# Two conv tiles instead of three by accumulating transfers, and most weight remainders on GpSimd

## Chip, core and metric

The kernel runs on one core of one Trainium2 chip. The metric is device time in microseconds (us) of one execution; the figure for the kernel is the median of three runs. A core has five engines with queues of their own: TensorE (PE in the profile; PEld is its loading of weights), VectorE (DVE), ScalarE (ACT), GpSimd (POOL) and SyncE (SP, which issues transfers here). An engine takes its instructions in the order in which the program gives them and waits, on semaphores, for what they need.

## What is computed

One layer of a decoder trunk on a sequence of 1024 tokens of width 1024, in float32:

```python
h = rmsnorm(x, norm_g[l]) * (1.0 + scale[:, None, :]) + shift[:, None, :]
u = h @ w_in[l]
cv, cg, cs, lx, ls = jnp.split(u, [D_CONV, 2*D_CONV, 3*D_CONV, 3*D_CONV + D_LRU], axis=-1)

v = cv * jax.nn.sigmoid(cg)
v = causal_depthwise_conv(v, dw_w[l], dw_b[l])            # 31 taps
v = jax.nn.silu(layernorm(v, cln_g[l], cln_b[l]))         # over all 1024 channels
y_conv = (v @ pw2_w[l] + pw2_b[l]) * jax.nn.silu(cs)
...
y = jnp.concatenate([y_conv, y_lru], axis=-1) @ w_out[l]
x = x + (1.0 + gate[:, None, :]) * y
return rmsnorm(x, final_g)
```

The left-out part is the second group: a 4-tap conv, two gates from block-diagonal products, and a linear recurrence over the tokens. `scale`, `shift` and `gate` come from a product of the condition `c` with `mod_w`.

## The kernel before

**Tiles.** Channels lie on the 128 partitions and tokens along the free axis, so a tensor of 1024 channels is eight tiles of 128 x 1024. Products use the fast float32 format of TensorE in three parts: each operand is split into a rounded value (`h`, by a cast on ScalarE) and what is left of it (`l`, by a subtraction), and TensorE adds h·h, h·l and l·h. For a weight tile these are `whi` and `wlo`. The subtraction that makes `wlo` is the *remainder* of the title. One weight tile of the middle takes 48 matmuls of 512 columns.

**Stages.** First the modulation and the products of the first four weight tiles (`first`), then the other 36 tiles of `w_in` mixed with the eight heads' gates, then the eight recurrence tiles of `w_out` (`lru`), while the LayerNorm of the conv group runs beside them; then the pointwise product (`pw2`, a scheme of seven products for eight) and the rest of `w_out`, and the final norm. TensorE's share of the conv group begins only with `pw2`, after the LayerNorm.

**Order.** No engine's order is written by hand. `Plan.op` collects each operation with an engine, an estimated cost and a priority (lower first); `Plan.order` plays them through one clock: whenever an engine is free it takes the ready operation with the lowest priority. The order in which they were taken is then emitted and is fixed. The planner also models that VectorE and GpSimd share a port: `o.lock` marks every GpSimd operation that is no transfer, and every VectorE operation that doesn't read PSUM; two such operations are not put at the same time (`held`). An operation's `lock` on VectorE is `not in_psum(r)` (L371, L377).

**Weights.** `weights` (L496) loads a weight tile with priority n - 2.5 and hands it to `w_slice` (L479), which casts it on ScalarE and subtracts with `SUB` (L384, a `TT`, L373) with priority n - 1.4, n being the tile's number. `whi` and `wlo` have two buffers each, so a tile can be prepared once TensorE has finished the one before the last. Tiles below `EARLY` = 11 that aren't in `LOP` have their remainder on GpSimd (these are 8, 9 and 10), the others on VectorE.

**Conv tiles.** `conv_tile` (L1085, priority 1000 + 5i, behind everything else) makes the 31 taps by a scheme of even and odd positions with 15, 14 and 14 plus 1 multiply-adds (`STT`, L366), each with one operand in SBUF and the accumulator (`cacc`, `caccs`) in PSUM, on VectorE. A tile whose number is in `POOLED` goes to `conv_pooled` (L1136) instead: ScalarE makes the products (`cq`, `co`), and GpSimd adds them up by transfers that accumulate in memory (`ADD`, L379, into `es` and `oo`). Both forms end with three additions of half tiles on VectorE. `conv_sum` (L1172) adds the eight results to `csum`, in the order 2, 6, 1, 4, 3, 0, 7, 5, and not before weight tile 38 has begun; the LayerNorm starts from it.

The rule by which the order is found, at its core (L248):

```python
k = (o.prio + (2.0 if o.table and o.table != table else 0.0), o.seq)
if key is not None and k >= key:
    continue
```

Of the kernel before, what the change touches and what calls it, by code (L numbers as in the profile page):

```python
# [9 lines left out]
F32 = mybir.dt.float32  # L10
F32R = mybir.dt.float32r
AF = mybir.ActivationFunctionType
ALU = mybir.AluOpType
# [31 lines left out]
ZK = 3  # L45
UK = 7
HRES = 6
POOLED = (1, 3, 5)
TLATE = 2
QGATES = ((2, 5), (3, 0), (3, 2), (3, 2))  # L50
CSUM = 38
# [30 lines left out]
SP0 = 1.0  # L82
SPP = 25
PAD = 16
GLO = 'DVE'
GDOT = 'DVE'
FOLD = 'DVE'
# [28 lines left out]

class Op:
    __slots__ = ("eng", "cost", "emit", "prio", "table", "bufs", "succ", "wait", "ready",
                 "seq", "reserve", "columns", "lock", "end", "psum", "lag", "slack")


class Plan:
# [23 lines left out]
    def op(self, eng, cost, emit, prio, r=(), w=(), table=None, after=(), reserve=0,  # L146
           columns=0, lock=False, lag=0.0, slack=0.0):
        o = Op()
        o.lag, o.slack = lag, slack
        o.eng, o.cost, o.emit, o.prio, o.table = eng, cost, emit, prio, table  # L150
        o.succ, o.ready, o.seq, o.reserve = [], 0.0, len(self.ops), reserve
        o.columns = columns
        o.lock = not lag and eng == "POOL" or eng == "DVE" and lock
        r, w = list(self.keys(r)), list(self.keys(w))
        preds = set(after)
        for k in r:
            if k in self.writer:
                preds.add(self.writer[k])
        for k in w:
            if k in self.writer:  # L160
                preds.add(self.writer[k])
            preds.update(self.readers.get(k, ()))
        for k in r:
            self.readers.setdefault(k, []).append(o)
        for k in w:
            self.writer[k] = o
            self.readers[k] = []
        preds.discard(o)
        o.wait = len(preds)
        for p in preds:  # L170
            p.succ.append(o)
        o.bufs = list(dict.fromkeys(k[0] for k in r + w if isinstance(k[0], Buf)))
        for b in o.bufs:
            b.left += 1
        o.psum = [(b, any(k[0] is b for k in w)) for b in o.bufs if b.pool == "bank"]
        self.ops.append(o)
        return o

    def order(self):
# [10 lines left out]
        waiting = None  # L190
        left = len(self.ops)

        def clear(o):
# [36 lines left out]
        while left:  # L230
            while releases and releases[0][0] <= t:
                free[heapq.heappop(releases)[2]] += 1
            moved, later = False, []
            if waiting and held["DVE"] <= t + 1e-9:
                o, waiting, moved = waiting, None, True
                held["POOL"] = t + o.cost
                done(o, t + o.cost)
            for e in engines:
                if until[e] > t + 1e-9:
                    continue  # L240
                best, key = None, None
                for o in pending[e]:
                    if o.ready > t + 1e-9:
                        continue
                    if e == "DVE" and o.lock and held["POOL"] > t + 1e-9:
                        later.append(held["POOL"])
                        continue
# [12 lines left out]
                    best, key = o, k  # L260
                if best is None:
# [12 lines left out]
                end = t + cost  # L274
                out.append((t, o))
                for b in o.bufs:
                    if b.pool in free and b not in live:
                        live.add(b)
                        free[b.pool] -= 1
                if e == "POOL" and o.lock and held["DVE"] > t + 1e-9:  # L280
                    waiting, until[e] = o, float("inf")
                    continue
                if o.lock:
                    if e == "DVE":
                        end = max(t, held["POOL"]) + cost
                    held[e] = end
                done(o, end)
            if not moved:
                nxt = later + [u for u in until.values() if t + 1e-9 < u < float("inf")]
                nxt += [o.ready for e in engines for o in pending[e] if o.ready > t + 1e-9]  # L290
                if releases:
                    nxt.append(releases[0][0])
                assert nxt, "no operation can go on"
                t = min(nxt)
        return out

    def run(self):
        for _, o in self.order():
            for b in o.bufs:
                if b.tile is None:  # L300
                    pool, tag, shape, _ = self.pools[b.pool]
                    b.tile = pool.tile(shape, b.dtype, tag=tag, name=b.name)
            o.emit()


@with_exitstack
def hymba_layer(ctx: ExitStack, tc: tile.TileContext, xT, xa, vecs, mod_w, mod_s0, w_first, w_pairs, w_in,
# [21 lines left out]
    for n in ("u", "s", "s2", "q", "r"):  # L329
        pools["sp_" + n] = (small, "sp_" + n, [P, KT], 1)  # L330
    S = Plan(pools)


    def a_cost(n, ptr=0):
# [30 lines left out]

    def STT(prio, out, in0, scalar, in1, op0, op1, n=T, accum=None, r=(), w=(), after=()):  # L366
        def emit():
            dve.scalar_tensor_tensor(out=out(), in0=in0(), scalar=scalar, in1=in1(), op0=op0,  # L368
                                     op1=op1, accum_out=accum)
        return S.op("DVE", d_cost(n, not isinstance(scalar, float)), emit, prio, r, w,  # L370
                    lock=not in_psum(r), after=after)  # L371

    def TT(prio, eng, out, a, b, op, n=T, r=(), w=(), reserve=0, after=()):  # L373
        e = dve if eng == "DVE" else pool
        return S.op(eng, d_cost(n) if eng == "DVE" else p_cost(n),
                    lambda: e.tensor_tensor(out=out(), in0=a(), in1=b(), op=op), prio, r, w,  # L376
                    reserve=reserve, lock=not in_psum(r), after=after)  # L377

    def ADD(prio, out, a, n=T, r=(), w=(), after=()):  # L379

        return S.op("POOL", ISSUE, lambda: pool.dma_start(out(), a(), accum_op=ALU.add), prio, r,  # L381
                    w, lag=RATE * n / T, after=after)

    def SUB(prio, eng, lo, full, hi, n=T, r=(), w=(), reserve=0):  # L384
        return TT(prio, eng, lo, full, lambda: hi().bitcast(F32), ALU.subtract, n, r, w, reserve)
# [683 lines left out]
    def tap_sums(pr):  # L1069
        def emit():  # L1070
            t = V[:, DWW:].rearrange("p (i s) -> p i s", s=TAPS)[:, :, 1:]
            t = t.rearrange("p i (q z) -> p i q z", z=2)
            dve.tensor_tensor(out=wsum.rearrange("p (i q) -> p i q", q=15), in0=t[:, :, :, 0],
                              in1=t[:, :, :, 1], op=ALU.add)
# [583 lines left out]
```

## Time and profile before

| | |
|---|---|
| median of three runs | 726.26 us (726.0 to 726.36) |
| the profiled execution: span from first to last instruction | 724.4 us |
| instructions | 8887 |
| TensorE busy | 717.0 us, 99% |
| VectorE busy | 638.9 us, 88% |
| ScalarE busy | 474.2 us, 65% |
| GpSimd busy | 86.6 us, 12% |
| mean granted TensorE clock | 0.997 |
| TensorE's stages, by the chain that ended last | first weights 8.4 to 47 us; middle to 557; pointwise 557 to 633; output to 718 |
| bytes by GpSimd's transfer queue | 34.26 MB of 111.58 MB |

The span is of one execution, and the time of a run is somewhat longer than it (by 1.9 us here). "Busy" is the union of an engine's instructions; those of TensorE overlap, as a matmul of 512 columns is shown with 389 ns while one begins every 227 ns. A row of a group reads: line, engine, operation, output <- inputs, shapes, count | busy us, mean ns | idle time of the engine before them <- what ended it. Lines are often those of a helper (L368 is `STT`, L376 `TT`, L357 and L349 `ACT`, L381 `ADD`).

### The profile page before, as it was taken

What the parts mean: (1) busy time and instruction counts of PE and PEld (TensorE: products, weight loads), DVE (VectorE), ACT (ScalarE), POOL (GpSimd) and SP (SyncE); (2) the same over time, 40 slices, a digit from 0 to 9 for tenths busy, and PEclk for the clock granted to TensorE, in tenths of its full rate; (3) what the DMA queues carried; (4) which work ended last, traced back from release to release, by engine and by line L of the source; (5) the groups of instructions that cost most, each with busy time, mean ns of one, the idle gap of its engine ahead of it and who ended that gap; (6) DMA issues with size and microseconds to landing.
All of it is one profiled execution on the core that took longest, in us unless ns stands there. A gap on an engine that the chain in (4) does not pass through costs nothing.

```text
span 724.4 us, 8887 instructions
## 1 busy us (share of the span) xinstructions
PE 717.0 (99%) x3236; PEld 596.9 (82%) x3236; DVE 638.9 (88%) x907; ACT 474.2 (65%) x659; POOL 86.6 (12%) x101
## 2 busy tenths in 40 slices
PE   9999999999999999999999999999999999999996
PEld 7888888888888888888888888888888888888886
DVE  6999999999999988688899995998999766997757
ACT  6675765777787977957867895835764334645443
POOL 0001012121231332233121100000000000000001
PEclk9999999999999999999999999999999999999998
DMA  9960024397799799799884536243332530433116
GB/s 342 407 234 29 30 92 104 83 202 181 172 237 235 149 216 222 148 217 210 187 178 90 105 89 195 88 175 138 124 117 86 205 111 6 159 108 140 59 57 233
DMA packets 36475, 111.58 MB, mean 154 GB/s; under 512 B 4048, under 2 KB 10960, under 8 KB 36432
## 3 DMA queue, kind: packets, MB, share of 16 engines
q1 hardware_dynamic: 23616, 76.36, 29.3%
q0 software_dynamic: 12528, 34.26, 26.3%
q8 instruction: 25, 0.41, 0.2%
q10 hardware_dynamic: 288, 0.39, 0.1%
q14 instruction: 18, 0.15, 0.1%
HBM read 64.16 MB, written 12.58 MB: 106 GB/s over the span
## 4 chain that ended last, share of the span: by engine, by line
PE 99%; DVE 0%; ACT 0%; issue 0%; DVEq 0%
PE ps L508 66%; PE first L807 5%; PE pupw L619 3%; PE papw L619 3%; PE gate L1247 3%; PE pbpw L619 3%; PE out L689 2%; PE puout L619 2%; PE paout L619 2%; PE pcpw L619 2%; PE pb0out L619 1%; PE pcout L619 1%; PE late L807 1%; PE out6b L689 1%; PE c_row L759 1%; PE pb1out L619 0%
## 5 line engine op out<-in xcount | busy, mean ns | idle before, releaser
L508 PE MATMUL ps<-uh,whi 128*128 128x512 f32 x576 | 224.2, 389 | 0.0
L508 PE MATMUL ps<-ul,whi 128*128 128x512 f32 x576 | 224.1, 389 | 0.0
L508 PE MATMUL ps<-uh,wlo 128*128 128x512 f32 x576 | 224.1, 389 | 0.0
L508 PEld LDWEIGHTS ps<-uh,wlo 128*128 128x128 f32 x576 | 108.1, 188 | 22.5
L508 PEld LDWEIGHTS ps<-ul,whi 128*128 128x128 f32 x576 | 108.1, 188 | 22.4
L508 PEld LDWEIGHTS ps<-uh,whi 128*128 128x128 f32 x576 | 108.1, 188 | 22.3
L349 ACT CAST whi<-raw 128x1024 fp32r<-128x1024 f32 x46 | 48.1, 1049 | 41.8 <-PE ps L508 34.7
L376 DVE TENSOR_TENSOR wlo<-raw,whi 128x1024 fp32r<-128x1024 f32 x43 | 52.5, 1221 | 17.0 <-ACT whi L349 16.7
L357 ACT ACT_TABLE_LOAD x47 | 60.3, 1283 | 3.6 <-issue 1.5
L381 POOL DMA_DIRECT2D es<-cq x45 | 40.3, 908 | 165.8 <-ACT cq L357 118.5
L368 DVE SCALAR_TENSOR_TENSOR cacc<-v,V,cacc 128x511 f32<-128x511 f32 (+14 forms) x75 | 55.8, 744 | 0.4
L368 DVE SCALAR_TENSOR_TENSOR caccs<-v,V,caccs 128x511 f32<-128x511 f32 (+6 forms) x70 | 52.2, 745 | 1.2
L368 DVE SCALAR_TENSOR_TENSOR caccs<-c,wsum,caccs 128x511 f32<-128x511 f32 (+6 forms) x70 | 52.1, 745 | 0.6
L508 PE MATMUL ps<-yh,wlo 128*128 128x512 f32 x128 | 49.8, 389 | 0.0
L508 PE MATMUL ps<-yl,whi 128*128 128x512 f32 x128 | 49.8, 389 | 0.0
L508 PE MATMUL ps<-yh,whi 128*128 128x512 f32 x128 | 49.8, 389 | 0.0
L381 POOL DMA_DIRECT2D oo<-co x42 | 38.7, 921 | 82.5 <-ACT co L357 39.6
L368 DVE SCALAR_TENSOR_TENSOR xs<-ps,V,xs 128x512 f32<-128x512 f32 (+3 forms) x48 | 35.9, 747 | 0.8 <-ACT xs L357 0.5
L376 POOL TENSOR_TENSOR fg<-fg,bc 128x512 f32<-128x512 f32 x2 | 2.5, 1278 | 276.9 <-ACT bc L349 276.9
L357 ACT ACTIVATE cq<-v,V 128x511 f32<-128x511 f32 (+14 forms) x45 | 31.8, 708 | 0.0
L357 ACT ACTIVATE cq<-c,wsum 128x512 f32<-128x512 f32 x42 | 29.6, 714 | 0.0
L357 ACT ACTIVATE co<-v,V 128x511 f32<-128x511 f32 (+13 forms) x42 | 29.4, 708 | 0.0
(387 smaller groups left out, 1441.9 us busy)
## 6 DMA issues: line engine op xcount, KB each, us to landing
raw<-in_w_in_dram SPq DMA_DIRECT2D x36, 512.0 KB, 5.1
modw<-in_mod_w_dram SPq DMA_DIRECT2D x23, 512.0 KB, 8.8
raw<-in_w_out_dram SPq DMA_DIRECT2D x10, 512.0 KB, 4.0
scsd<-scs SPq DMA_DIRECT2D x8, 512.0 KB, 4.0
acc<-in_xT_dram SPq DMA_DIRECT2D x8, 512.0 KB, 4.4
accd<-acc SPq DMA_DIRECT2D x8, 512.0 KB, 2.6
rawpw<-in_pw_dram SPq DMA_DIRECT2D x8, 512.0 KB, 3.2
scsr<-scsd SPq DMA_DIRECT2D x8, 512.0 KB, 4.9
```

The costliest lines, as they stand in the source:

```text
L349: act.copy(out(), in_())
L357: act.activation(out=out(), in_=in_(), func=func, **kw)
L368: dve.scalar_tensor_tensor(out=out(), in0=in0(), scalar=scalar, in1=in1(), op0=op0, op1=op1, accum_out=accum)
L376: lambda: e.tensor_tensor(out=out(), in0=a(), in1=b(), op=op), prio, r, w,
L381: return S.op("POOL", ISSUE, lambda: pool.dma_start(out(), a(), accum_op=ALU.add), prio, r, w, lag=RATE * n / T, after=after)
L508: pe.matmul(part(ps, a - off, b - off)(), k3(lhs)()[:, k, :], rhs[k]()[:, a:b], start=(k == 0 and lhs is wh and rhs is xh and (a - off) % ...
L619: pe.matmul(part(ps, 0, c1 - c0)(), half(*lhs)()[:, j * P:j * P + P], half(*rhs)()[:, c0:c1], start=start and j == 0 and z == 0, stop=j == ...
L689: pe.matmul(part(ps, a - off, e - off)(), k3(lhs)()[:, k, :], rhs()[:, i * H + a % H:i * H + a % H + e - a], start=k == KORD[0] and lhs is ...
L759: pe.matmul(part(ps_c[z], k * P - a, k * P - a + P)(), cs[:, k:k + 1].to_broadcast([P, P]), ident, start=True, stop=True)
L807: pe.matmul(part(ps, a - off, b - off)(), fw_part(lhs, k, i * P, i * P + P)(), rhs()[:, a:b], start=k == 0 and lhs is wh and rhs is xh, st ...
L1247: pe.matmul(ps(), lhs()[:, j, :], rhs()[:, c0:c1], start=st == 0, stop=st == 2)
```

## The change

`POOLED` becomes (2, 4): conv tiles 1, 3 and 5 go to VectorE, 2 and 4 to the transfers. The remainders whose preparation priority lies from 6 to 46 are marked `pooled` with GpSimd's cost. When the planner picks for VectorE, such an operation counts as one that GpSimd may take: for the first 5 us after it is ready VectorE leaves it alone, and GpSimd gets it as soon as GpSimd is free, VectorE's next operation is one that reads PSUM, and the PSUM-reading work at hand lasts at least 0.7 of GpSimd's cost. It is then made to wait for the VectorE operation before that stretch (`behind`, a dependency for the order alone). After the 5 us VectorE may take it as before.

```diff
-POOLED = (1, 3, 5)
+POOLED = (2, 4)
...
+DEFER, RUNS = 5.0, 0.7
+PW0, PW1 = 6, 46
+SYNC = mybir.DependencyInfo(mybir.DependencyClass.Sync, mybir.DependencyReason.SCHED_ONLY)
...
 class Op:
...
+    def run(self):
+
+        n, o = 0.0, self
+        while o is not None:
+            n += o.cost
+            o = next((s for s in o.succ if s.eng == "DVE" and not s.lock and s.wait == 1), None)
+        return n
...
-                best, key = None, None
+                best, key, flex, run = None, None, [], 0.0
                 for o in pending[e]:
                     if o.ready > t + 1e-9:
                         continue
+                    if o.pooled and held["POOL"] <= t + 1e-9:
+                        flex.append(o)
+                        if t + 1e-9 < o.ready + DEFER:
+                            later.append(o.ready + DEFER)
+                            continue
...
                     best, key = o, k
+                    if e == "DVE" and not o.lock:
+                        run += o.run()
+                if flex and best is not None and not best.lock and until["POOL"] <= t + 1e-9 \
+                        and not waiting:
+                    o = min(flex, key=lambda o: (o.prio, o.seq))
+                    if run >= RUNS * o.pooled:
+                        o.eng, o.cost, o.behind = "POOL", o.pooled, previous
+                        pending[e].remove(o)
...
+                        held["POOL"] = t + o.cost
+                        done(o, t + o.cost)
...
+                if e == "DVE":
+                    previous = o
...
-            o.emit()
+            o.ins = o.emit()
+            if o.behind:
+                self.tc.add_manual_dep(o.ins.ins, o.behind.ins.ins.name, SYNC, reason="shared port")
...
-    def TT(prio, eng, out, a, b, op, n=T, r=(), w=(), reserve=0, after=()):
+    def TT(prio, eng, out, a, b, op, n=T, r=(), w=(), reserve=0, after=(), pooled=False):
+        def emit():
+            return (dve if o.eng == "DVE" else pool).tensor_tensor(out=out(), in0=a(), in1=b(), op=op)
...
+        if pooled and eng == "DVE":
+            o.pooled = p_cost(n)
+        return o
...
-        SUB(LOP.get(p_load + 2.5, p_prep), eng, cut(lo), cut(rw), cut(hi), n, r=keys(rw) + keys(hi), w=keys(lo))
+        SUB(LOP.get(p_load + 2.5, p_prep), eng, cut(lo), cut(rw), cut(hi), n, r=keys(rw) + keys(hi),
+            w=keys(lo), pooled=PW0 <= p_prep <= PW1)
```

The rest of the diff lets the helpers return the instruction that they emit.

More of the change, by code (lines that the diff above doesn't have):

```diff
@@ L118 @@
     __slots__ = ("eng", "cost", "emit", "prio", "table", "bufs", "succ", "wait", "ready",
-                 "seq", "reserve", "columns", "lock", "end", "psum", "lag", "slack")
+                 "seq", "reserve", "columns", "lock", "end", "psum", "lag", "slack", "pooled",
+                 "behind", "ins")
+    def run(self):
[4 more added lines that the diff above has]
+        return n
 class Plan:
@@ L148, in op @@
         o = Op()
-        o.lag, o.slack = lag, slack
+        o.lag, o.slack, o.pooled, o.behind, o.ins = lag, slack, None, None, None
         o.eng, o.cost, o.emit, o.prio, o.table = eng, cost, emit, prio, table
@@ L189, in order @@
         held = {"DVE": 0.0, "POOL": 0.0}
-        waiting = None
+        waiting, previous = None, None
         left = len(self.ops)
@@ L260, in order @@
                     best, key = o, k
+                    if e == "DVE" and not o.lock:
[6 more added lines that the diff above has]
+                        pending[e].remove(o)
+                        left -= 1
+                        out.append((t, o))
+                        for b in o.bufs:
+                            if b.pool in free and b not in live:
+                                live.add(b)
+                                free[b.pool] -= 1
+                        held["POOL"] = t + o.cost
+                        done(o, t + o.cost)
                 if best is None:
@@ L331, in hymba_layer @@
     S = Plan(pools)
+    S.tc = tc
     def a_cost(n, ptr=0):
@@ L367, in emit @@
         def emit():
-            dve.scalar_tensor_tensor(out=out(), in0=in0(), scalar=scalar, in1=in1(), op0=op0,
-                                     op1=op1, accum_out=accum)
+            return dve.scalar_tensor_tensor(out=out(), in0=in0(), scalar=scalar, in1=in1(),
+                                            op0=op0, op1=op1, accum_out=accum)
         return S.op("DVE", d_cost(n, not isinstance(scalar, float)), emit, prio, r, w,
                     lock=not in_psum(r), after=after)
-    def TT(prio, eng, out, a, b, op, n=T, r=(), w=(), reserve=0, after=()):
[L374 to L377, printed above, removed]
+    def TT(prio, eng, out, a, b, op, n=T, r=(), w=(), reserve=0, after=(), pooled=False):
+        def emit():
+            return (dve if o.eng == "DVE" else pool).tensor_tensor(out=out(), in0=a(), in1=b(), op=op)
+        o = S.op(eng, d_cost(n) if eng == "DVE" else p_cost(n), emit, prio, r, w,
+                 reserve=reserve, lock=not in_psum(r), after=after)
+        if pooled and eng == "DVE":
+            o.pooled = p_cost(n)
+        return o
     def ADD(prio, out, a, n=T, r=(), w=(), after=()):
```

9 lines of the change are left out of this document (5 added, 4 removed).

## The prediction

> **What bounds the kernel now.** I read the table of windows first, cut where TensorE's state changes: before its first large product, the long middle, the last products, and what follows them. Columns: the window, its length, then busy time and instructions of PE, PEld, DVE, ACT and POOL, the granted TensorE clock, the DMA share and GB/s.
>
> ```profile
> 0.00:8.40 8.40, 6.80 (x31) 6.43 (x31) 2.95 (x14) 4.71 (x9) 0.70 (x6) 1.00 0.77 260
> 8.40:700.00 691.60, 691.60 (x3057) 572.55 (x3058) 618.74 (x859) 458.11 (x621) 83.36 (x93) 1.00 0.56 152
> 700.00:718.30 18.30, 18.30 (x151) 17.88 (x149) 14.63 (x30) 11.34 (x31) 2.53 (x2) 1.00 0.38 142
> 718.30:724.40 6.10, 0.27 (x3) 0.08 (x1) 2.55 (x5) 0.00 (x0) 0.00 (x0) 0.70 0.72 266
> sum 724.40, PE 716.97 PEld 596.93 DVE 638.87 ACT 474.15 POOL 86.59; mean PE 179.24 PEld 149.23 DVE 159.72 ACT 118.54 POOL 21.65
> ```
>
> The reader is to see that TensorE is busy for all of the 691.60 us of the middle, at clock 1.00, and then for all 18.30 us of the last products. "Busy" alone would not prove it, since the ends of matmuls are modelled, so the second view is that of the waits of PE, with the sum, the number and the longest:
>
> ```profile
> PE token_stats L754 <- DVE ones L441: 1.1, 1, 1.1
> PE first L807 <- ACT fhi L349: 0.5, 1, 0.5
> ```
>
> Only two waits are listed, 1.6 us together, both before the middle begins. Nothing that VectorE, GpSimd or a DMA does between 8.4 and 700 us makes TensorE wait. **The kernel is bound by the number of matmuls.** The change adds none, removes none and leaves their sizes. What another order of the other engines could win lies in the first 8.4 us and the last 6.1 us, and neither the conv tiles nor the remainders with a preparation priority of 6 to 46 run there. VectorE at 88% looks like a second bound, but an engine with no one waiting for it can give up work without shortening anything.
>
> **The change part by part.** The rows of the page's groups that carry the sizes (count, busy time, mean of one in ns, idle before it):
>
> ```profile
> L376 DVE TENSOR_TENSOR wlo<-raw,whi 128x1024 fp32r<-128x1024 f32 x43 | 52.5, 1221 | 17.0 <-ACT whi L349 16.7
> ...
> L368 DVE SCALAR_TENSOR_TENSOR cacc<-v,V,cacc 128x511 f32<-128x511 f32 (+14 forms) x75 | 55.8, 744 | 0.4
> L368 DVE SCALAR_TENSOR_TENSOR caccs<-v,V,caccs 128x511 f32<-128x511 f32 (+6 forms) x70 | 52.2, 745 | 1.2
> L368 DVE SCALAR_TENSOR_TENSOR caccs<-c,wsum,caccs 128x511 f32<-128x511 f32 (+6 forms) x70 | 52.1, 745 | 0.6
> ...
> L357 ACT ACTIVATE cq<-v,V 128x511 f32<-128x511 f32 (+14 forms) x45 | 31.8, 708 | 0.0
> ```
>
> And GpSimd's own groups, with shapes kept apart:
>
> ```profile
> L381 POOL DMA_DIRECT2D es<-cq x45 | 40.3, 908 | 165.8 <-ACT cq L357 118.5 <-DMA oo<-co 20.3 <-issue 11.5
> L381 POOL DMA_DIRECT2D oo<-co x42 | 38.7, 921 | 82.5 <-ACT co L357 39.6 <-issue 11.1 <-DMA es<-cq 10.6
> L376 POOL TENSOR_TENSOR wlo<-raw,whi 128x1024 fp32r<-128x1024 f32 x3 | 7.2, 2408 | 98.4 <-ACT whi L349 98.4
> ```
>
> *1. One conv tile more on VectorE.* The loop of `conv_tile` issues 15+15+14 multiply-adds a tile, the odd one of which (`caccs<-c,V`) is in a smaller group: 44 x 0.745 = 32.8 us added to VectorE. The four whole-tile passes around them (the sum of even and odd positions and three folds) exist in both forms of the tile: 0.
>
> *2. One tile fewer by accumulating transfers.* GpSimd issues 15 + 14 = 29 fewer of them: 15 x 0.908 + 14 x 0.921 = 26.5 us off GpSimd, and a third of that queue's bytes go. ScalarE loses the 47 products of a tile and gains 3 starts of an accumulator: 44 x 0.708 = 31.2 us off. Both engines were off the path, so the sum takes nothing for this; the cover is TensorE's gapless middle.
>
> *3. Remainders to GpSimd.* `weights` makes remainders 7 to 47 in the main loop; 8 to 10 are on GpSimd already, 7 has a preparation priority of 5.6 and stays, so 37 may move. Each takes 1.22 us from VectorE and costs GpSimd 2.41 us: at most 45.1 us off and 89.1 us on. GpSimd then holds 86.6 - 26.5 + 89.1 = 149 us of 724: no bound. A planner rule sends a remainder back to VectorE when it has waited 5 us, so I take 25 to 33 as moved.
>
> *VectorE's balance.* What matters is the time up to the channel sum that the LayerNorm needs. Windows by the arrivals of conv tiles, then the sum row of the same windows for the tile wlo alone:
>
> ```profile
> 98.00:248.00 150.00, 150.00 (x664) 124.20 (x663) 145.75 (x222) 111.85 (x149) 34.90 (x39) 1.00 0.69 162
> 248.00:362.00 114.00, 114.00 (x505) 94.39 (x504) 92.89 (x121) 88.61 (x124) 32.83 (x38) 1.00 0.95 199
> 362.00:438.00 76.00, 76.00 (x337) 62.94 (x336) 75.38 (x93) 58.09 (x75) 13.12 (x15) 1.00 0.54 116
> 438.00:477.00 39.00, 39.00 (x174) 32.30 (x173) 30.49 (x29) 26.37 (x30) 0.00 (x0) 1.00 0.48 152
> ```
>
> ```profile
> sum 379.00, PE 204.46 PEld 98.53 DVE 37.85 POOL 4.82; mean PE 51.12 PEld 24.63 DVE 9.46 POOL 1.21
> ```
>
> VectorE idles 4.25 + 21.11 + 0.62 + 8.51 = 34.5 us there, and does 37.85 us of remainders. With all moved the balance is 32.8 - 37.9 = -5 us; with three quarters, +4 us; with none, +32.8 us, which the idle time would still just hold. The timeline shows what the sum waited for:
>
> ```profile
> 438.06 1.28 DVE L376 TENSOR_TENSOR c<-c,caccs 128x512 f32<-128x512 f32 x2
> ...
> 476.03 1.22 DVE L376 TENSOR_TENSOR csum<-csum,c 128x1024 f32<-128x1024 f32 x1
> ```
>
> VectorE's last tile was done at 439; the sum ended at 477 because tile 5 came late by the transfers. Now tile 5 is VectorE's and the transfers carry 2 and 4, which arrive earlier, so I expect the sum at 455 to 477. An earlier sum moves work to other places of a middle that TensorE fills anyway: 0. What is late next is again the matmul count.
>
> *4. The added wait.* Each moved remainder waits on GpSimd behind a VectorE instruction. Behind it in GpSimd's order stand the accumulating transfers' issues and later remainders; for the former only tiles 2 and 4 wait, for the latter TensorE. This is where the change can cost, and these rows give the room: a cast, the remainder that follows it, the first matmul with it.
>
> ```profile
> 201.41 1.05 ACT L349 CAST whi<-raw 128x1024 fp32r<-128x1024 f32 x1 [4.43 <-PE ps L508]
> ...
> 212.77 0.39 PE L508 MATMUL ps<-uh,wlo 128*128 128x512 f32 x1
> ...
> 432.61 1.06 ACT L349 CAST whi<-raw 128x1024 fp32r<-128x1024 f32 x1 [0.39 <-PE ps L508]
> ...
> 436.92 1.22 DVE L376 TENSOR_TENSOR wlo<-raw,whi 128x1024 fp32r<-128x1024 f32 x1
> ...
> 470.37 1.06 ACT L349 CAST whi<-raw 128x1024 fp32r<-128x1024 f32 x1
> ...
> 479.33 0.39 PE L508 MATMUL ps<-yh,wlo 128*128 128x512 f32 x1
> ```
>
> From the end of a cast (202.46) to the first use (212.77) there are 10.3 us; in the tightest place I found (471.43 to 479.33) 7.9. The planner lets a remainder wait up to 5 us, and GpSimd needs 2.4: 7.4 at worst, which leaves 2.9 us typically and 0.5 at the tightest place. On top comes how far the chip runs behind the plan: the remainder at 436.92 began 3.3 us after its cast although its priority is high, because VectorE's fixed order had other work first. The bounds of this step are therefore 0 (no remainder late) and about 3.3 - 0.5 = 2.8 us (the tightest one late by the largest lag). It is no sum over remainders: TensorE, once delayed, delays the next use as well, so only the largest excess counts. I take 0, since it needs a full wait, the tightest place and the largest lag together.
>
> *5. GpSimd beside VectorE.* The planner keeps the two apart unless VectorE reads PSUM. The one case of before inside a stretch of VectorE work:
>
> ```profile
> 54.78 3.67 DVE L376 TENSOR_TENSOR first_u<-first,rbc 128x512 f32<-128x512 f32 x6
> ...
> 55.66 2.40 POOL L376 TENSOR_TENSOR wlo<-raw,whi 128x1024 fp32r<-128x1024 f32 x1 [54.36 <-ACT whi L349]
> ```
>
> Six instructions in 3.67 us (0.61 apiece) while GpSimd took its usual 2.40: neither slowed, and `first` is in PSUM. The conv multiply-adds too have one operand in PSUM and one in SBUF, so I price the overlap at 0. No row shows GpSimd beside a VectorE instruction with both operands in SBUF; bounds: 0, and one whole remainder, 2.4 us of VectorE, each time. [...]
>
> **Sum.** 0 + 0 + 0 + 0 + 0 on the profiled execution: span 724.4 us. The median of the runs is 726.26, so 1.86 us lie around the span, and I leave them: **726.3 us**.
>
> **Rivals.**
>
> *A. A remainder comes late (slower).* GpSimd's queue holds a remainder behind an issue that waits for ScalarE's product (those waits are the 118.5 us of the row above), and TensorE waits for it. For: the reserve of 0.5 to 2.9 us against a lag of up to 3.3. Against: ScalarE loses 31 us of work and a third of the issues go. It decides from the point where wait + lag pass 7.9 us at the tightest or 10.3 us at the usual place. Price 1.6 to 4 us: 728 to 730.
>
> *B. GpSimd and VectorE exclude each other often (slower).* If the real order drifts, each moved remainder can stop VectorE for up to 2.4 us. VectorE has 34.5 us of room, less the balance of -5 to +4: from about 13 to 16 full stops on, the channel sum passes 477 and TensorE runs dry before the pointwise products. At 18 stops, 43 us, it is 4 to 13 us over: 730 to 739. [...]
>
> *C. The end is laid out anew (faster).* The planner is one pass over all operations, so another state at 560 us could reorder the last 24 us. There TensorE leaves 6.1 - 0.27 = 5.8 us; were a quarter of it and the 0.5 us wait won, 724.3. Against: of the 72.9 us that VectorE idles in the middle window (691.60 - 618.74) at most 34.5 lie between 98 and 477 us; in the rest, most of it after the channel sum, a difference of the two orders should have died out.
>
> *D. Few remainders move.* If the planner seldom finds the PSUM stretch, VectorE carries the tile alone: +32.8 against 34.5 us of room. The time is again 726.3, with the sum later.
>
> **How the numbers follow.** Forecast 0.62 and D 0.10 both stay within 0.2% (1.45 us; about what a measurement can tell): same 0.72. A 0.15 and B 0.06: slower 0.21. C: faster 0.07. The range reaches from 725.2, a little under the lowest run (726.0), to 729.5, which takes in most of A; left out are B, C and the end of A, about 0.16. The likeliest case's own range is 725.6 to 727.2.
>
> **What would show it.** Right: PE's waits still list no more than the two at the start, the middle window still 691.6 of 691.6, while wlo shows 28 to 36 instructions on POOL at about 2.4 us, the conv groups grow to 90, 84 and 84, and the issues fall to 30 and 28. Wrong by A: a wait of PE on POOL wlo. By B: wlo on POOL, or VectorE's two-operand groups, with means well over 2.4 and 1.22 us, and the sum later than 477. By C: a shorter stretch after 700 us with the same middle.

## The result, and the profile after

On one chip, nine runs of each: 725.83 us before (725.48 to 726.36), **727.74 us after** (727.68 to 728.35). The ratio is 1.0026, with a 95% interval of 1.0018 to 1.0035: slower by 1.9 us, just over what a measurement of this kernel can tell from no change. The time lies in the predicted range, on the side to which I had given 0.21. One run of the kernel before (801 us) and two of a kernel below (802 and 1037 us) came out far longer at a lower granted clock (0.85, 0.85 and 0.65) and are left out of all medians and ratios here.

What was meant to move did move. The page of after, first its busy line, then its groups:

```profile
PE 716.0 (99%) x3236; PEld 595.6 (82%) x3236; DVE 647.0 (89%) x923; ACT 447.5 (62%) x615; POOL 137.5 (19%) x99
...
L413 POOL TENSOR_TENSOR wlo<-raw,whi 128x1024 fp32r<-128x1024 f32 x31 | 85.1, 2744 | 276.8 <-ACT whi L387 103.3
...
L406 DVE SCALAR_TENSOR_TENSOR cacc<-v,V,cacc 128x511 f32<-128x511 f32 (+14 forms) x90 | 66.7, 741 | 0.5
L406 DVE SCALAR_TENSOR_TENSOR caccs<-v,V,caccs 128x511 f32<-128x511 f32 (+6 forms) x84 | 62.5, 743 | 1.3
L406 DVE SCALAR_TENSOR_TENSOR caccs<-c,wsum,caccs 128x511 f32<-128x511 f32 (+6 forms) x84 | 62.5, 744 | 1.1
...
L422 POOL DMA_DIRECT2D oo<-co x28 | 28.1, 1003 | 42.6 <-ACT co L395 14.1
L422 POOL DMA_DIRECT2D es<-cq x30 | 29.2, 997 | 9.8 <-DMA es<-cq 7.5
```

(The diff shifts the lines: `TT` is now L413, `STT` L406, `ADD` L422.) The conv groups are 90, 84 and 84, the issues 30 and 28, and 28 remainders more are on GpSimd, 31 in all. One number is off: a remainder took 2.408 us on GpSimd before, and the mean is now 2.744. The tile wlo with shapes kept apart (minimum, median, maximum in ns) says that this is no general slowing:

```profile
L413 POOL TENSOR_TENSOR wlo<-raw,whi x31: 2393/2407/4293, 55.0 to 460.5; 128x1024 fp32r<-128x1024 f32 x31
```

The median is the old 2.41; a few took 4.29. The waits of PE (total, times, longest) and the windows of after, cut as before, show what came of it:

```profile
PE mean L1347 <- DVE meanl L413: 1.6, 1, 1.6
PE first L850 <- DVE uh L432: 1.1, 1, 1.1
PE token_stats L797 <- DVE ones L483: 1.1, 1, 1.1
```

```profile
8.40:700.00 691.60, 690.02 (x3051) 570.96 (x3050) 625.48 (x873) 430.41 (x575) 134.28 (x91) 1.00 0.48 136
700.00:718.30 18.30, 18.30 (x148) 17.87 (x146) 14.84 (x30) 11.48 (x30) 2.52 (x2) 1.00 0.34 128
```

There is one new wait, in the middle that had none, and it is the whole gap of the middle window: 691.60 - 690.02 = 1.58 us. No wait on wlo is listed. (The wait at `first` is longer than before, but `first` begins at 7.74 us and not at 8.36, so nothing is lost there.) The profiled span is 725.9 against 724.4 us, 1.5 more; the 1.9 us between the medians are of the same size. So the question is what made `meanl` late. It is the remainder of the channel sum, an operand of the matmul `mean` with which the LayerNorm starts. The timeline of after (start, duration) at that place:

```profile
457.93 1.22 DVE L413 TENSOR_TENSOR csum<-csum,c 128x1024 f32<-128x1024 f32 x1
...
460.32 2.29 DVE L1303 TENSOR_TENSOR_SCAN r<-a,xs 128x1024 f32<-128x1024 f32 x1
...
460.51 4.29 POOL L413 TENSOR_TENSOR wlo<-raw,whi 128x1024 fp32r<-128x1024 f32 x1 [13.78 <-ACT meanh L387]
...
462.53 3.36 DVE L413 TENSOR_TENSOR meanl<-csum,meanh 128x1024 fp32r<-128x1024 f32 x1
...
463.96 0.40 PE L1347 MATMUL mean<-meanh,minus_r 128*128 128x512 f32 x1
465.94 0.50 PE L1347 MATMUL mean<-meanl,minus_r 128*128 128x512 f32 x1 [1.58 <-DVE meanl L413]
```

And the same place before:

```profile
478.37 1.23 DVE L376 TENSOR_TENSOR meanl<-csum,meanh 128x1024 fp32r<-128x1024 f32 x1 [1.12 <-ACT meanh L349]
...
480.47 0.39 PE L1304 MATMUL mean<-meanl,minus_r 128*128 128x512 f32 x1
```

The reader is to see a chain of three. VectorE's scan, the recurrence over the tokens, runs. GpSimd's remainder starts 0.2 us into it and is shown with 4.29 us; 2.4 us before its end is 462.4, about where the scan ends. `meanl` starts there in turn and takes 3.36 us where 1.23 is usual; 1.2 us before its end is 464.7, about where GpSimd ends. As I read it, each waits out the other; the trace lists no wait of either for the other, and the extra time (1.88 and 2.13 us) is part of the durations. Before the change `mean` came 0.87 us after `meanl` (480.47 - 479.60), so a hold of 2.1 us could not be hidden. In the changed order the room is smaller still: unheld, `meanl` would end at 462.53 + 1.22 = 463.75, and its matmul would begin one spacing behind the other at 463.96 + 0.23 = 464.19. A hold of 2.14 us less 0.44 of room makes 1.70; the matmul begins 465.94 - 464.19 = 1.75 us late.

Why did GpSimd start beside a scan, which reads two operands from SBUF? The description of the planner above says that every VectorE operation that doesn't read PSUM is marked `lock`. That is not quite so: the scan is entered by a direct call without the mark.

```python
S.op("DVE", 2.2, lambda: dve.tensor_tensor_scan(
    out=r(), data0=a(), data1=xs(), initial=0.0, op0=ALU.mult, op1=ALU.add),
    pr, [a, xs], [r])
```

To the new rule it is therefore PSUM work of 2.2 us, more than 0.7 of GpSimd's 2.4. Five of the 31 remainders begin in a scan (at 136.95, 240.46, 295.84, 364.15 and 460.51 us); the other four hold an `sls` instead of `meanl`, one of them here:

```profile
295.64 2.29 DVE L1303 TENSOR_TENSOR_SCAN r<-a,xs 128x1024 f32<-128x1024 f32 x1
...
295.84 4.29 POOL L413 TENSOR_TENSOR wlo<-raw,whi 128x1024 fp32r<-128x1024 f32 x1 [7.05 <-DVE xs L413]
...
297.97 3.25 DVE L413 TENSOR_TENSOR sls<-sls,r 128x1024 f32<-128x1024 f32 x1
```

No matmul waits for those.

### The profile page after: what moved, and what is told of

It reads as the page before. It is cut to its first block, busy times and chain, and to the rows that moved or that the text cites. A ratio compares the mean times of both kernels' runs of the same rounds, so it can differ in the third digit from the quotient of the medians.

```text
span 725.9 us, 8818 instructions
## 1 busy us (share of the span) xinstructions
PE 716.0 (99%) x3236; PEld 595.6 (82%) x3236; DVE 647.0 (89%) x923; ACT 447.5 (62%) x615; POOL 137.5 (19%) x99
## 4 chain that ended last, share of the span: by engine, by line
PE 95%; DVE 3%; ACT 1%; DMA 1%; issue 1%; DVEq 0%; SPq 0%; ACTq 0%
PE ps L551 63%; PE first L850 5%; PE pbpw L662 3%; PE pupw L662 3%; PE papw L662 3%; PE gate L1290 3%; PE out L732 2%; PE puout L662 2%; PE paout L662 2%; PE pcpw L662 1%; DVE csum L413 1%; PE pb0out L662 1%; PE pcout L662 1%; PE late L850 1%; PE out6b L732 1%; DMA modw<-in_mod_s_dram 1%
## 5 line engine op out<-in xcount | busy, mean ns | idle before, releaser
L413 POOL TENSOR_TENSOR wlo<-raw,whi 128x1024 fp32r<-128x1024 f32 x31 | 85.1, 2744 | 276.8 <-ACT whi L387 103.3
L406 DVE SCALAR_TENSOR_TENSOR cacc<-v,V,cacc 128x511 f32<-128x511 f32 (+14 forms) x90 | 66.7, 741 | 0.5
L406 DVE SCALAR_TENSOR_TENSOR caccs<-v,V,caccs 128x511 f32<-128x511 f32 (+6 forms) x84 | 62.5, 743 | 1.3
L406 DVE SCALAR_TENSOR_TENSOR caccs<-c,wsum,caccs 128x511 f32<-128x511 f32 (+6 forms) x84 | 62.5, 744 | 1.1
L413 POOL TENSOR_TENSOR fg<-fg,bc 128x512 f32<-128x512 f32 x2 | 2.5, 1282 | 250.7 <-ACT bc L387 250.7
L406 DVE SCALAR_TENSOR_TENSOR xs<-ps,V,xs 128x512 f32<-128x512 f32 (+3 forms) x48 | 35.8, 745 | 0.7 <-ACT xs L395 0.5
L422 POOL DMA_DIRECT2D oo<-co x28 | 28.1, 1003 | 42.6 <-ACT co L395 14.1
L422 POOL DMA_DIRECT2D es<-cq x30 | 29.2, 997 | 9.8 <-DMA es<-cq 7.5
L406 DVE SCALAR_TENSOR_TENSOR modw<-modw,sc 128x1024 f32<-128x1024 f32 x23 | 27.9, 1219 | 0.9 <-DMA modw<-in_mod_w_dram 0.9
L551 PEld LDWEIGHTS ps<-yh,wlo 128*128 128x128 f32 x128 | 24.0, 188 | 5.0
L551 PEld LDWEIGHTS ps<-yh,whi 128*128 128x128 f32 x128 | 24.0, 188 | 5.0
```

The lines of the kernel that those rows point to most:

```text
L406: return dve.scalar_tensor_tensor(out=out(), in0=in0(), scalar=scalar, in1=in1(), op0=op0, op1=op1, accum_out=accum)
L413: return (dve if o.eng == "DVE" else pool).tensor_tensor(out=out(), in0=a(), in1=b(), op=op)
L551: pe.matmul(part(ps, a - off, b - off)(), k3(lhs)()[:, k, :], rhs[k]()[:, a:b], start=(k == 0 and lhs is wh and rhs is xh and (a - off) % ...
```

## The experiments

In the expectations P is the theory just read from the trace, that the collision at the scan costs the time ("port" is the planner's word for what it models; the traces show the durations and no cause of them), and W the rival that the added waits of GpSimd behind VectorE do. D is the prediction's rival D. Other letters are the cases that an expectation sets out itself. Ratios are to the kernel before on the same chip, with 95% intervals.

### The waits taken away

```diff
-            if o.behind:
+            if False:
```

> The changed kernel in its order, without the dependency of a GpSimd remainder on the VectorE instruction before its stretch. Theory P: GpSimd then begins as soon as the cast is there, so collisions come at other places and possibly more of them; the time depends on whether one meets meanl: with the same order of instructions the remainder by mean would begin 1 to 3 us earlier, before or in the scan; I expect 4 or more remainders over 3 us and a ratio of 0.999 to 1.003. Rival W expects the loss gone (0.999 to 1.001) because the waits are gone, whatever the collisions do.

738.91 us, ratio 1.0175 (1.0158 to 1.0193): outside the range of P as well as of W. The orders of all engines are those of after. Thirteen VectorE operations, two scans among them, now take 1.6 to 2.4 us longer than others of their kind, and seven remainders on GpSimd take more than 3 us. PE's three largest waits, and a collision in the reverse order from the timeline:

```profile
PE mean L1347 <- DVE meanl L413: 2.9, 1, 2.9
PE ps L551 <- DVE wlo L413: 1.8, 1, 1.8
PE ps L551 <- POOL wlo L413: 1.6, 2, 1.3
```

```profile
304.85 3.15 POOL L413 TENSOR_TENSOR wlo<-raw,whi 128x1024 fp32r<-128x1024 f32 x1 [5.18 <-ACT whi L387]
...
305.78 4.37 DVE L1303 TENSOR_TENSOR_SCAN r<-a,xs 128x1024 f32<-128x1024 f32 x1
```

Here GpSimd was first, and it is the scan that takes 4.37 us instead of 2.29. W falls: without the waits the kernel is 11 us slower than with them. They keep apart instructions that lengthen each other (here GpSimd's 3.15 us for 2.41 and the scan's 4.37 for 2.29). P had the collisions, but not how many there would be or that TensorE would then wait for remainders too.

### The one remainder beside `meanl` back on VectorE

```diff
-PW0, PW1 = 6, 46
+PW0, PW1 = 6, 38
```

> The changed kernel with the range of preparation priorities cut from 46 to 38, so that the last remainders (numbers 40 to 47, among them the one beside meanl) stay on VectorE. The order before about 440 us should be the same, with its four other collisions. Theory P: those four cost nothing, because nothing that TensorE waits for is near; the PE wait at mean falls below 0.3 us and the ratio is 0.999 to 1.001. Rivals L and W: mean stays late (VectorE has more work, not less), ratio 1.0015 to 1.003.

726.01 us, ratio 0.9998 (0.9989 to 1.0007). Exactly one remainder left GpSimd (30 remain), and the wait at `mean` went, while the other four collisions stay, as P had it. The timeline of this run:

```profile
458.74 1.22 DVE L413 TENSOR_TENSOR wlo<-raw,whi 128x1024 fp32r<-128x1024 f32 x1
...
464.34 1.20 DVE L413 TENSOR_TENSOR meanl<-csum,meanh 128x1024 fp32r<-128x1024 f32 x1
```

All of the 1.9 us are gone, and four collisions cost nothing. But the planner also laid out VectorE's order anew from 458 us on and TensorE's from 464, so this run alone doesn't show that the collision was the cause; the kernels below that keep the order do.

### Only the matmul `mean` planned later

```diff
-        S.op("PE", 0.91, mean_mm, -1, [mh, ml], mean.b)
+        S.op("PE", 0.91, mean_mm, -1, [mh, ml], mean.b, slack=4.0)
```

> The changed kernel, but the matmul of the channel mean is planned 4 us later (slack on its inputs), so that TensorE's order has other matmuls first. The five collisions stay or move little. If the wait at mean is all that the change costs, the time goes back to that of the kernel before (ratio 0.999 to 1.001), with remainders of 4.2 us still in the profile. If the time is lost elsewhere as well (W: TensorE waiting for remainders; or a longer end), 1.001 to 1.003 is left.

727.08 us, ratio 1.0016 (1.0007 to 1.0025): not back to the time before, as it would be if the wait at `mean` were all. All five collisions stay, and the wait at `mean` is gone, but PE's waits show another:

```profile
PE lnss L1330 <- ACT hilnss L387: 0.3, 1, 0.3
PE lnss L1330 <- DVE lolnss L413: 0.2, 1, 0.2
```

`lnss` is the next matmul of the LayerNorm. What its matmuls take there beyond TensorE's usual spacing of 0.23 us comes to 1.2 us, more than the 0.5 us of listed waits. (This profile also has about 2 us lost at the start, where the granted clock was 0.57 from 8.3 to 12.3 us; they are no part of the 1.2.)

### The same remainder on GpSimd, but behind `meanl`

At the emission, the remainder of weight tile 40 is taken out of its place and put behind `meanl` (in `one.behind` too); the rest of every order is that of after.

```diff
+        i, j = ops.index(one), ops.index(rest)
+        ops.insert(j + 1, one)
+        del ops[i]
+        one.behind = rest
```

> The changed kernel with the same operations on the same engines and the same orders; only the GpSimd remainder of weight tile 40, which began 0.2 us into the last scan, waits behind meanl instead. VectorE's, ScalarE's and TensorE's orders are those of the changed kernel. Theory P (the collision with meanl is the whole loss): meanl takes 1.22 us and ends near 463.8 us, no PE wait at mean or lnss over 0.3 us, the remainder ends near 466.3 us against its first use at 468 to 469, four other remainders still take 4.2 to 4.3 us, ratio 0.999 to 1.001. Rival L (mean is late in the changed order whatever GpSimd does) keeps 1 us or more at mean and 1.0015 to 1.003. It also separates P from the reading that the kernel without this remainder on GpSimd was saved by another order of VectorE.

727.28 us, ratio 1.0027 (1.0018 to 1.0036): no gain. The timeline shows why (lines shifted by 9; the `yl` row holds three instructions, the first of 3.44 us):

```profile
462.38 1.20 DVE L422 TENSOR_TENSOR meanl<-csum,meanh 128x1024 fp32r<-128x1024 f32 x1
463.50 1.22 DVE L422 TENSOR_TENSOR sls<-sls,r 128x1024 f32<-128x1024 f32 x1
464.63 5.71 DVE L422 TENSOR_TENSOR yl<-sls,yh 128x1024 fp32r<-128x1024 f32 x3
...
463.71 3.27 POOL L422 TENSOR_TENSOR wlo<-raw,whi 128x1024 fp32r<-128x1024 f32 x1 [17.12 <-PE ps L560]
```

`meanl` is on time at 1.20 us, but the collision has moved on by one instruction, from `meanl` to `yl`, and VectorE is late by as much. The same waits at `lnss` (0.3 and 0.2 us) and the same 1.2 us there: from the last matmul ahead of the four of `lnss` to the first behind them it is 2.36 us, against 1.15 before (505.45 to 506.60).

```profile
495.16 0.39 PE L560 MATMUL ps<-yh,wlo 128*128 128x512 f32 x1
...
497.52 0.39 PE L560 MATMUL ps<-yh,whi 128*128 128x512 f32 x1
```

"The collision with `meanl`" was too narrow: what counts is that VectorE loses about 2 us between the channel sum and `lnss`; the first matmul on the way that has no room shows it.

### The same place, on VectorE

As the last, but with `one.eng, one.behind = "DVE", None`.

> As the kernel with the remainder of tile 40 behind meanl, but VectorE itself does it there (1.22 us) instead of GpSimd; all else in the same order. With GpSimd doing it, VectorE's next two-operand instruction took 3.44 us instead of 1.22, so VectorE lost 2.2 us, and TensorE 1.2 us at lnss. Theory S: what counts is how far VectorE falls behind the plan between the channel sum and lnss; now it loses 1.2 us there instead of 2.2, so the loss at lnss falls from 1.2 to about 0.2 us, ratio 1.000 to 1.001. Rival L (the chain to lnss is late by itself in the changed order): 1 us or more stays at lnss, ratio 1.0015 to 1.003.

726.18 us, ratio 1.0003 (0.9994 to 1.0012). VectorE does the remainder at that place, which delays what follows by 1.2 us instead of 2.2, and the loss at `lnss` falls from 1.2 to 0.1 us (1.29 us between the same two matmuls). PE's waits list only the two of the start.

```profile
495.44 0.39 PE L560 MATMUL ps<-yh,wlo 128*128 128x512 f32 x1
...
496.73 0.39 PE L560 MATMUL ps<-yh,whi 128*128 128x512 f32 x1
```

This is the cleanest pair: the two kernels differ in the engine of one instruction (and its wait), and all other instructions keep their order; their intervals (1.0018 to 1.0036, and 0.9994 to 1.0012) don't meet.

### Both matmuls planned later

The edit at `mean`, and the same slack for the matmul of `lnss`:

```diff
-        S.op("PE", 2 * (n + 32) / 2400, total, pr, [hi, lo], [ps], columns=2 * n)
+        S.op("PE", 2 * (n + 32) / 2400, total, pr, [hi, lo], [ps], columns=2 * n,
+             slack=4.0)
```

> The changed kernel with the matmuls of mean and of lnss both planned 4 us later, so that TensorE's order has other matmuls first; every remainder stays on GpSimd with its collisions. Theory S: the loss came only from these two places of TensorE's order, which had under 1 us of room, so it is gone: no PE wait but those at the start, five remainders of 4.2 to 4.3 us still there, ratio 0.999 to 1.001. Rival: the later LayerNorm shows up at the pointwise product instead (as in the kernels whose channel sum came after 484 us), with PE waits at papw or pbpw and 1.0015 or more. Neither expects less than the time before.

725.81 us, ratio 1.0001 (0.9993 to 1.001). The timeline keeps the collision whole:

```profile
460.29 4.30 POOL L413 TENSOR_TENSOR wlo<-raw,whi 128x1024 fp32r<-128x1024 f32 x1 [13.80 <-ACT meanh L387]
...
462.30 3.37 DVE L413 TENSOR_TENSOR meanl<-csum,meanh 128x1024 fp32r<-128x1024 f32 x1
```

With 4 us of slack at two matmuls, and not one remainder moved, the change costs nothing. This shows where the 1.9 us are lost; and that nothing is won either, since the matmuls set the time again.

### The scan marked, or only PSUM readers admitted

Two ways to close the hole in the rule:

```diff
-            pr, [a, xs], [r])
+            pr, [a, xs], [r], lock=True)
```

```diff
-                if flex and best is not None and not best.lock and until["POOL"] <= t + 1e-9 \
+                if flex and best is not None and best.psum and until["POOL"] <= t + 1e-9 \
```

> The changed kernel, but the planner is told that the scan reads SBUF alone (lock), so no remainder may be put beside it. Theory P (port): in the changed kernel five remainders began 0.2 us into a scan, took 4.2 to 4.3 us instead of 2.4, and held up the next VectorE instruction with two SBUF operands by 1.6 to 2.1 us; the fifth of these was the channel sum's remainder meanl, whose matmul stood 0.4 us behind it in the plan, so TensorE stood still for 1.75 us. P expects: every remainder on GpSimd at 2.4 to 2.8 us, meanl at 1.22 us, no wait of PE at mean over 0.3 us, and the time of the kernel before, ratio 0.999 to 1.001. Rival L (load): VectorE and ScalarE run behind the plan at the channel sum because of the additional conv tile, and mean is late in any order; L expects a PE wait at mean of 1 us or more, ratio 1.0015 to 1.003. Rival W (the added waits): GpSimd's waits behind VectorE cost the time wherever the remainders stand; W expects 1.0015 to 1.003 as well, with remainders late.

> The scan-locked kernel again, for an undisturbed profile. P had expected the time of before and was wrong by 5 us. Rival L: the waits of PE stand at the pointwise product (papw, pbpw on vla, vlb), 4 to 6 us together, none at mean; the last conv tile ends after 470 us and the channel sum after 475 (439 and 477 before), since 24 and not 28 remainders were moved and VectorE may not scan beside them. Time 730.5 to 731.6.

> The changed kernel, but a remainder goes to GpSimd only if the VectorE operation picked for that moment itself uses PSUM, so a scan can no longer be the cover; the scan is otherwise planned as in the change (it may begin beside a running remainder). Theory P: the remainders that begin 0.2 us into a scan are gone, none is held for 4.2 us at the scan's start; the wait at mean of 1.6 us is gone if no other collision meets it, ratio 0.999 to 1.001. Rival L: with fewer remainders moved (under 31) VectorE falls behind as in the scan-locked kernel, the last conv tile and the LayerNorm come late: 1.003 to 1.008, with PE waits at the pointwise product.

The mark gave 731.12 us, ratio 1.0068 (1.0055 to 1.0081), and in a second set of runs 731.1 and 1.0067 (1.0048 to 1.0085). The other gave 731.32 and 1.0064 (1.0051 to 1.0076). P had expected the time of before and was wrong; the rival L of the two later expectations had the time and the place of the waits. Of the collisions with a scan none is left, as the tile wlo of the second set shows; but there are 27 remainders on GpSimd and not 31:

```profile
L413 POOL TENSOR_TENSOR wlo<-raw,whi x27: 2390/2404/2757, 55.3 to 472.3; 128x1024 fp32r<-128x1024 f32 x27
```

The other four are VectorE's again, and the planner's orders differ from those of after from 137 us on. In the PSUM-only run the last conv tile and the sum come at these times, and then the pointwise products wait:

```profile
480.45 1.28 DVE L413 TENSOR_TENSOR c<-c,caccs 128x512 f32<-128x512 f32 x2
481.77 2.48 DVE L413 TENSOR_TENSOR csum<-csum,c 128x1024 f32<-128x1024 f32 x2
```

```profile
PE pbpw L662 <- ACT vha L387: 1.1, 1, 1.1
...
PE papw L662 <- DVE vlb L413: 0.7, 1, 0.7
PE pbpw L662 <- DVE vla L413: 0.7, 1, 0.7
```

The channel sum ends at 484.3 us, in the marked run at 484.7, against 459.2 after and 477.3 before. Four remainders more are 4.9 us of VectorE's work, and the sum is 25 us later, while VectorE idles 36.6 us between 98 and 477 us against 24.1 after. So it isn't the added work alone; which wait in the new order makes the tile late was not tested. The three waits make 2.5 us; about 6 are lost in all. The windows of the PSUM-only run show most of the rest:

```profile
564.00:570.00 6.00, 3.54 (x12) 1.79 (x11) 6.00 (x9) 2.91 (x5) 0.00 (x0) 0.86 0.06 23
570.00:575.00 5.00, 5.00 (x13) 3.90 (x12) 4.96 (x8) 0.59 (x1) 0.00 (x0) 0.50 0.01 3
```

After a stretch in which TensorE was busy for 3.54 of 6.00 us, its granted clock is 0.50 for five microseconds; a matmul began every 0.43 us instead of every 0.23, about 2.5 us more.

### Each half alone

Conv tiles changed, no remainder offered to GpSimd; and remainders moved, with tiles 1, 3 and 5 by transfers as before:

```diff
-            w=keys(lo), pooled=PW0 <= p_prep <= PW1)
+            w=keys(lo), pooled=False)
```

```diff
-POOLED = (2, 4)
+POOLED = (1, 3, 5)
```

> Half of the change: conv tiles 2 and 4 by transfers, but no remainder is marked for GpSimd (8, 9 and 10 stay there as before). VectorE gets 32.8 us more and nothing off. The prediction's rival D, by the 34.5 us of room, expects no change in the time (ratio 0.999 to 1.001) with the channel sum later. Rival L, since the scan-locked kernel lost 5 us with its last conv tile late, expects the sum and with it the LayerNorm late and TensorE waiting for the pointwise product's operands: ratio 1.005 to 1.02, PE waits at papw or pbpw. No remainder over 2.8 us on either.

> The other half: remainders on GpSimd by the new rule, conv tiles 1, 3 and 5 by transfers as before. VectorE loses up to 38 us of work before the channel sum. Theory P expects collisions beside scans again (3 to 8 remainders over 3.5 us), and a cost only where one holds up an operand that TensorE takes at once; otherwise ratio 0.999 to 1.001. Rival W (the waits and remainders on GpSimd cost by themselves) expects 1.0015 to 1.003.

**The conv tile alone** costs 17.8 us: 743.93 us, ratio 1.0252 (1.0236 to 1.0269). The windows of this run, to be read against those of before with the same bounds:

```profile
98.00:248.00 150.00, 150.00 (x664) 124.24 (x663) 146.42 (x222) 107.26 (x141) 29.46 (x32) 1.00 0.62 147
248.00:362.00 114.00, 114.00 (x504) 94.44 (x503) 102.66 (x138) 77.30 (x107) 23.50 (x27) 1.00 0.75 161
362.00:438.00 76.00, 76.00 (x337) 62.95 (x336) 70.96 (x87) 49.27 (x59) 2.61 (x3) 1.00 0.24 64
438.00:477.00 39.00, 39.00 (x174) 32.31 (x173) 37.52 (x42) 23.75 (x27) 0.00 (x0) 1.00 0.38 138
```

VectorE had 32.8 us more to do and still idles 3.6 + 11.3 + 5.0 + 1.5 = 21.4 us there, out of 34.5: it could use only 13 us of its idle time by 477. The rest of the tile ran behind it, the sum ended at 500.0 us, and the pointwise products waited (2.7 us for `pupw`, 2.0 for `vla`, 2.0 for `vlb`, 1.7 for `vha`); the granted clock, 1.00 in the windows from 98 to 545 us, was 0.92 on the mean from 545 to 590 us. Before them TensorE also waited 2.7 us for a weight's remainder, `wlo`, at 548.8 us. L had the mechanism, and at 1.02 too small an upper end.

**The remainders alone** cost 8.7 us: 734.83 us, ratio 1.0117 (1.0101 to 1.0133), outside what both theories had expected. Six remainders collide with a scan, and GpSimd's queue has the last of tile 5's transfers behind one of them. The timeline of this run's GpSimd:

```profile
463.10 4.29 POOL L413 TENSOR_TENSOR wlo<-raw,whi 128x1024 fp32r<-128x1024 f32 x1 [6.82 <-DVE xs L413]
...
467.93 1.20 POOL L422 DMA_DIRECT2D es<-cq  x1
```

and the last such issue before:

```profile
436.63 0.89 POOL L381 DMA_DIRECT2D es<-cq  x1 [3.46 <-DMA es<-cq]
```

The last issue comes 31 us later, and the sum ends at 491.9. By the starts of its matmuls the profile's 8.7 us (733.1 against 724.4) lie in three places. About 2.0 are at the start, where the granted clock was 0.59 from 8.3 to 12.5 us. 2.7 are between 471 and 478 us, where matmuls wait four times for `yl`, whose `sls` was held to 3.25 us by the remainder shown. 3.5 are at the pointwise products behind the late sum. PE's wait for `yl`, and the window of the pointwise products:

```profile
PE ps L551 <- DVE yl L413: 1.3, 4, 0.8
```

```profile
570.00:576.00 6.00, 3.44 (x13) 1.96 (x13) 6.00 (x9) 2.77 (x4) 0.00 (x0) 1.00 0.00 1
```

PE waits there 1.1 us for `vha`, 0.65 for `vla` and 0.79 for `vlb`, much as in the PSUM-only run, and is as little busy, but here the granted clock stays at 1.00.

So the halves cost 17.8 and 8.7 us, and together 1.9. Each hides most of the other's cost: the remainders make room on VectorE for the conv tile (the sum ends at 459.2 and not at 500.0), and with one tile fewer GpSimd's last accumulating transfer is issued at 377.9 and not at 467.9 us.

## Why the prediction was nearly right, and where it was wrong

**The bound held.** TensorE is gapless in the middle but for the one wait, the matmul count is the same, and no version beat the kernel before. 0 was right as the upper limit of the gain.

**The sizes held.** The conv groups and the issues came exactly, the moved remainders (28) within 25 to 33. ScalarE lost 474.2 - 447.5 = 26.7 us (31.2 predicted). GpSimd rose to 137.5 us: 86.6 - 26.5 + 28 x 2.41 = 127.6, and five remainders of some 1.9 us too much. VectorE did not come out lighter: 638.9 + 32.8 - 34.2 + 9.3 = 646.8 (647.0 measured), the 9.3 us being the holds of its five instructions, which are shown as busy time. The channel sum ended at 459.2, within 455 to 477.

**Step 4 held, against rival A.** TensorE waits for no remainder of a weight, so none was late; the added waits protect more than they cost. Without them TensorE does wait 3.4 us for `wlo`.

**The step that failed is step 5**, "I price the overlap at 0", on the ground that the planner keeps the two engines apart unless VectorE reads PSUM. I took the mark from the rule for two helpers and didn't look for operations that are entered past them; the scan is. The upper bound that I gave, a whole remainder of 2.4 us of VectorE each time, was an estimate: the profile before the change shows no such stop, and the runs after it show 1.6 to 2.2 us. They show the later of the two held in both orders: GpSimd 4.29 us instead of 2.41 behind a scan, the scan 4.37 us instead of 2.29 behind GpSimd. For VectorE work that reads PSUM the 0 was right: the conv groups keep their means (741 to 744 ns, 744 and 745 before), and the other 26 remainders took 2.39 to 2.76 us.

**With it failed the ground of "an earlier sum ... : 0"**, that TensorE fills the middle anyway. The 0 itself holds where nothing is held (sum at 459.3 us, ratio 1.0003, with the remainder on VectorE behind `meanl`). But I looked at the room of the remainders (7.9 and 10.3 us) and not at that of the other operands of TensorE. `mean` has a priority of -1 and is planned for the moment at which its operands are ready, so its room was 0.87 us. The row was there to be read in the trace of before.

**Rival B had the mechanism and the wrong form.** It asked for 13 to 16 stops that add up until the sum is late. Five came, and four cost nothing; one was enough, as it fell between the sum and a matmul without room. A loss by collisions is no sum over collisions.

**Rival D was wrong**, and with it VectorE's balance: idle time of a window isn't room. The 34.5 us of idle were to hold the tile; 13 did, and "time unchanged" was 17.8 us slower. The balance came out for the change as a whole only because 28 remainders x 1.22 = 34.2 us left VectorE against the 32.8 us that came. **Rival C** did not show: TensorE is busy for all 18.3 us behind 700 us as before.

Open remains how much of the 3.5 us at the pointwise products in the remainders-alone run comes from the late transfers and how much from collisions, and why the sum is 25 us later where the scan is no cover.

## What to carry to other kernels

Where a compute bound is gapless, ask of every operand that the bounding engine takes how long it lies ready, not only of those that the change touches: here the operation planned with the highest priority had the least room, and 4 us of slack there and at `lnss` took the cost of all collisions away. A rule that lets two engines overlap is only as good as its list of what excludes what; go through every instruction that runs in the stretch, and look at the maximum of a group, not its mean. And a part of an engine's idle share is no room until the work that would fill it is there in time.

## What the runs showed of the hardware

- Where a remainder on GpSimd met VectorE work with two operands in SBUF, the profile of the changed kernel lists no wait of either for the instruction that it met: the extra time is in the durations (`meanl` 3.36 instead of 1.20 us, wlo 4.29 instead of 2.40). Moving a remainder to GpSimd beside two-operand work cost VectorE 1.6 to 2.2 us, more than the 1.22 that it saved.
- In the PSUM-only run the granted clock fell to 0.50 for about 5 us after three waits of 1.1, 0.65 and 0.68 us within four microseconds, in a stretch with TensorE busy for 3.54 of 6.00 us (59%); about 6 us were lost in all, 2.5 of them in the waits. In the remainders-alone run the granted clock was 1.00 with waits of 1.1, 0.65 and 0.79 us and TensorE busy for 3.44 of 6.00 us, and 3.5 us were lost. What decides between the two the runs do not show.
